# The opening of a two-block transformer kernel rebuilt: c cast by transposes, token-major sums of squares, one x block and one weight per step, matmuls of zeros

## The chip, the core and the metric

One core of a Trainium2 chip runs the whole program in one launch. Time is device microseconds of that core; lower is better. The core has five engines with their own instruction streams, each worked off in order: PE (TensorE: matmuls, with PEld for its weight loads), DVE (VectorE), ACT (ScalarE), POOL (GpSimd) and SP (SyncE, which here issues the DMAs). They wait for each other by semaphores.

## The reference, cut to what matters

Two transformer blocks on 512 tokens of width 1024, batch 1, float32. The opening is the head of the first block: the modulation from c, the first norm, and the first projection.

```python
c_act = jax.nn.silu(c)
mod = (c_act @ ada_w[l] + ada_b[l])[:, None, :]          # 1024 -> 6 * 1024
sh_t, sc_t, g_t, sh_c, sc_c, g_c = jnp.split(mod, 6, axis=-1)
h = rms_norm(x, tm_pre_g[l]) * (1.0 + sc_t) + sh_t       # x / sqrt(mean(x^2) + eps) * g
y = token_mixer(h, w_in[l], ...)                         # starts with h @ w_in
```

## The kernel before

Activations lie with features on the partitions: x is 8 blocks `x0[:, j]` of 128 features by 512 tokens. A float32 product is made of three matmuls of the fp32r type: weight and activation are each split into a high part (rounded, by an ACT copy) and a low part (the rest, by a DVE subtraction), and high times high, high times low and low times high are summed in PSUM (`mm3`, L130 to L133; 512 columns each).

The opening stands in the block `with tc.tile_pool(name="st")`. It has no normed x at first: the gain 1 + scale of the modulation is folded into x, the reciprocal root of the mean square is multiplied onto the results later. Ahead of the loop, c is loaded onto all 128 partitions (`cb`, a DMA of 512 KB from a 4 KB row) and put through Silu on ACT; `ccol` is Silu of c as columns, from the small table `vec`.

The first loop runs over the 8 blocks j of x. I call its parts by step:

- product j: one block of `ada` (block 8 + j, 512 KB, one of four `sraw` buffers) is multiplied by `cb` on DVE and summed along the row into one column of `mod` (L347);
- gain j: a one-column DVE instruction makes `gcols` from it (L393);
- high half j on ACT and low half j on DVE: x block j times its gain, split in two (`xg`, L394 and L395);
- weight split j: a 512 KB block of `w1` is split, its high part on ACT and its low part on DVE (L119, L120). Blocks 0 to 4 go through `sraw`, 5 to 7 through three `raw` buffers (`wload`);
- matmuls of step j: `steps` brings the accumulators of the first four weights (`NF = 4`) up to block j. Step 0 has 3 matmuls, step 1 has 9, step 2 has 15, step 3 has 21, step 4 has 12; steps 5 and 6 have no call of their own: their 24 matmuls are written together with step 7's 12, and the scheduler may put them earlier.

In steps 0 to 3 two blocks of x are loaded per step (`XSTEP`), each squared on ACT (L379) and, but for the first, added into `ssx` on DVE (L381): 7 adds of 512 columns. After step 3 the column sums of `ssx` are taken by matmuls (`colsum`, L240), `rsqrt` makes 1/root from them in 12 small DVE instructions after a copy, `rowcast` puts the 4 columns on all partitions by 4 transposes on PE, and an ACT copy brings that to SBUF as `rx`.

After the loop, DVE takes the four accumulators out of PSUM times `rx` (`gq`, `gk`, L411 and L413), and a second loop over j (L417 on) makes the true normed `h`: the shift from `ada` block j (on DVE, but for j = 1, which `ADA_PE` gives to PE as 8 plain float32 matmuls of one column, L422), the normed block `nt` = x times gain times `rx` (L428), its high half on ACT and low half on DVE (L429, L430), and 12 matmuls for four more weights, whose first is into bank `pb`.

The order within an engine is set by the tile framework's scheduler, by the order in which the code is written and by its priorities; it is fixed when the program is built. SP issues the DMAs in order, each when its buffer is free.

## Time and profile before

| | us |
|---|---|
| median of 3 runs | 1601.64 |
| lowest and highest run | 1598.73, 1603.09 |
| the profiled execution, its own time | 1603.05 |
| its span, first to last instruction | 1601.3 |

The profile is of one execution. The span is what the views below cut up; 1.75 us of that execution's time lie around it. A timeline row gives start and duration of an instruction on its engine, so the start of the next row shows its pitch (instructions overlap a little at their ends). What an engine waited for stands in brackets.

### The profile page before, as it was taken

Reading aid. Unit: us, or ns where it says so; the run is one execution under the profiler, and the core shown is the slowest. Engines: PE = TensorE matmul, PEld = TensorE weight load, DVE = VectorE, ACT = ScalarE, POOL = GpSimd, SP = SyncE. Lnnn points to the kernel's source line nnn. Section 1 sums busy time; section 2 is a strip of 40 time slices with the busy share of each in tenths; the row PEclk is TensorE's granted clock in tenths of the full one; section 3 lists DMA queues with packets and bytes.
Section 4 is the critical chain, followed back from the end, with each engine's and each line's share of the span. In section 5 each row is a group of like instructions: output and inputs, shape, how many; then the busy total and the mean of one; then the engine's idle time right before and its main releaser. Section 6 shows DMA issues by size and latency. Waiting matters only on the chain.

```text
span 1601.3 us, 20852 instructions
## 1 busy us (share of the span) xinstructions
PE 1568.9 (98%) x8015; PEld 1316.4 (82%) x8015; DVE 1083.4 (68%) x2066; ACT 677.5 (42%) x1040; POOL 15.9 (1%) x43
## 2 busy tenths in 40 slices
...
GB/s 305 170 53 67 106 115 187 184 170 153 177 169 17 79 97 100 92 100 91 96 134 187 75 66 89 83 93 27 79 152 59 80 100 98 92 104 81 98 113 53
DMA packets 50963, 175.91 MB, mean 110 GB/s; under 512 B 5920, under 2 KB 6192, under 8 KB 50864
## 3 DMA queue, kind: packets, MB, share of 16 engines
...
HBM read 172.46 MB, written 2.10 MB: 109 GB/s over the span
## 4 chain that ended last, share of the span: by engine, by line
PE 90%; DVE 5%; ACT 3%; DMA 1%; issue 1%; SPq 0%; ACTq 0%; DVEq 0%
PE acc L131 23%; PE acc L132 23%; PE acc L133 23%; PE acc L197 3%; PE acc L1340 3%; PE tp L1340 2%; PE pc L1250 1%; PE pa L197 1%; PE pc L197 1%; PE pb L197 1%; PE pb L1340 1%; PE pa L1340 1%; PE pc L1340 1%; DVE lo L120 1%; PE acc L157 1%
## 5 line engine op out<-in xcount | busy, mean ns | idle before, releaser
L120 DVE TENSOR_TENSOR lo<-raw,hi 128x1024 fp32r<-128x1024 f32 (+1 forms) x245 | 296.4, 1211 | 312.0 <-ACT hi L119 307.9
L131 PE MATMUL acc<-hh,hi 128*128 128x512 f32 x1208 | 474.3, 393 | 0.0
L133 PE MATMUL acc<-hh,lo 128*128 128x512 f32 x1208 | 473.1, 392 | 0.0
L132 PE MATMUL acc<-hl,hi 128*128 128x512 f32 x1208 | 473.1, 392 | 0.0
L119 ACT ACTIVATE hi<-raw 128x1024 fp32r<-128x1024 f32 (+1 forms) x245 | 257.1, 1050 | 471.1 <-PE acc L132 352.6
L131 PEld LDWEIGHTS acc<-hh,hi 128*128 128x128 f32 x1208 | 227.7, 189 | 48.9 <-issue 2.0
L132 PEld LDWEIGHTS acc<-hl,hi 128*128 128x128 f32 x1208 | 227.5, 188 | 48.6 <-issue 1.8
L133 PEld LDWEIGHTS acc<-hh,lo 128*128 128x128 f32 x1208 | 227.6, 188 | 47.5 <-issue 0.7
L131 PE MATMUL acc<-act_h,hi 128*128 128x256 f32 (+1 forms) x242 | 80.4, 332 | 0.0
L132 PE MATMUL acc<-act_l,hi 128*128 128x256 f32 (+1 forms) x242 | 80.2, 331 | 0.0
L133 PE MATMUL acc<-act_h,lo 128*128 128x256 f32 (+1 forms) x242 | 80.2, 331 | 0.0
L119 ACT ACTIVATE act_h<-ffe 128x512 fp32r<-128x512 f32 x44 | 27.7, 630 | 102.5 <-DVE ffe L968 102.5
L265 DVE SCALAR_TENSOR_TENSOR raw<-raw,cb 128x1024 f32<-128x1024 f32 x32 | 39.1, 1223 | 40.0 <-DMA raw<-in_ada_dram 40.0
L964 DVE SCALAR_TENSOR_TENSOR ffe<-acc,vec,ffe 128x510 f32<-128x510 f32 x82 | 61.2, 748 | 2.6
L967 ACT ACTIVATE ffe<-ffe 128x512 f32<-128x512 f32 x44 | 27.8, 631 | 79.5 <-DVE ffe L964 79.5
L962 DVE SCALAR_TENSOR_TENSOR ffe<-acc,vec,ffe 128x511 f32<-128x511 f32 x82 | 60.7, 742 | 0.0
L131 PEld LDWEIGHTS acc<-act_h,hi 128*128 128x128 f32 x242 | 46.0, 190 | 4.4
L133 PEld LDWEIGHTS acc<-act_h,lo 128*128 128x128 f32 x242 | 46.0, 190 | 4.3
L132 PEld LDWEIGHTS acc<-act_l,hi 128*128 128x128 f32 x242 | 46.0, 190 | 4.3
L120 DVE TENSOR_TENSOR act_l<-ffe,act_h 128x512 fp32r<-128x512 f32 x44 | 30.3, 690 | 26.5 <-ACT act_h L119 26.5
L808 DVE SCALAR_TENSOR_TENSOR cv<-u,vec,cv 128x512 f32<-128x512 f32 x60 | 43.8, 746 | 0.1
L197 PE MATMUL acc<-hl,hi 128*128 128x256 f32 x144 | 40.2, 285 | 0.0
...
## 6 DMA issues: line engine op xcount, KB each, us to landing
...
```

The source lines that it names most:

```text
L119: A.activation(hi, src, AF.Copy)
L120: V.tensor_sub(lo, src, hi.bitcast(F32))
L131: T.matmul(out, wh_, ah, start=start, stop=False)
L132: T.matmul(out, wh_, al, start=False, stop=False)
L133: T.matmul(out, wl_, ah, start=False, stop=stop)
L197: T.matmul(a, w_, x_, start=(k == 0 and n == 0 and half == 0), stop=(k == KT - 1 and n == 2 and half == 1), skip_group_check=True)
L265: V.scalar_tensor_tensor(raw, raw, 1.0, cb, op0=ALU.mult, op1=ALU.mult, accum_out=mod[:, i:i + 1])
L808: V.scalar_tensor_tensor(cv[:, j], u0[:, j, k:k + 512], htap[:, 2 * k + j:2 * k + j + 1], cv[:, j], op0=ALU.mult, op1=ALU.add)
L962: V.scalar_tensor_tensor(t[:, 1:512], acc[:, 0:511], vcol(taps, 44 + i), t[:, 1:512], op0=ALU.mult, op1=ALU.add)
L964: V.scalar_tensor_tensor(t[:, 2:512], acc[:, 0:510], vcol(taps, i), t[:, 2:512], op0=ALU.mult, op1=ALU.add)
L967: A.activation(e[0], e[0], AF.Silu)
L1340: T.matmul(o, act[a][:, k, t], w[:, n0:n1], start=(k == 0 and i == 0), stop=(k == KF - 1 and i == 2), skip_group_check=True)
```

## The change

- c: the 512 KB DMA of c is gone. Silu of c as columns (`ccol`) is put on all partitions by 8 transposes on PE, each of one column broadcast over 128, into banks `pb` and `pc`; one half is copied to `cb` by ACT, the other by DVE.
- Matmuls of zeros: `warm` issues 3 and 7 plain float32 matmuls of 256 columns of a zeroed tile, before and after the transposes as the code is written. As built, 5 stand ahead of the transposes and 5 behind them.
- Products 3 and 6 (`ada` blocks 11 and 14, added to `ADA_PE`) are made on PE as 8 one-column matmuls each (L414), and the gain reads PSUM.
- Sums of squares: a second copy of x with tokens on the partitions (`xr`, 4 DMAs of 512 KB) is squared on ACT with a sum along the row, in steps 2 to 5. The 8 squares on ACT, the 7 adds on DVE and the column sums on PE are gone. `rsqrt` and `rowcast` stand behind the loop.
- Each step loads one block of x and one of the weights, and the weight split is written ahead of the high and low half.

```diff
--- before.py
+++ after.py
@@ -48,9 +48,8 @@
        "sb0", "sc0", "sx0", "sb1", "sc1", "sx1"]
 NST = 8
 NF = 4
-XSTEP = (2, 2, 2, 2, 0, 0, 0, 0)
-WSTEP = (1, 1, 1, 1, 1, 1, 1, 1)
-ADA_PE = (1,)
+WARM = (3, 7)
+ADA_PE = (1, 11, 14)
 
 PUMP_P, PUMP_V0, PUMP_V1, PUMP_QK, PUMP_G = 4, 8, 10, 3, (0, 0, 0, 0, 0, 12, 12, 12)
 MT2 = ["ik", "iq0", "iq1", "iq2", "iq3", "p0", "p1", "p2", "p3", "v0", "v1", "v2", "v3",
@@ -350,19 +349,37 @@
 
         x0 = xp.tile([128, KT, 512], F32, tag="x", name="x0")
         xg = h
-        nc.sync.dma_start(out=cb, in_=io["c"].broadcast_to([128, D]))
+
+        zero = st.tile([128, 256], F32, name="zero")
+        G.memset(zero, 0.0)
+        idle = bank("tp")
+
+        def warm(n):
+            for _ in range(n):
+                T.matmul(idle[:, 0:256], zero[:, 0:128], zero, start=True, stop=True)
+
+        warm(WARM[0])
         nc.sync.dma_start(out=vec[:, 0:VSTART], in_=io["vec"][:, 0:VSTART])
-        A.activation(cb, cb, AF.Silu)
+        nc.sync.dma_start(out=ident, in_=io["cst"])
         ccol = sm.tile([128, KT], F32, tag="ccol", name="ccol", bufs=1)
         A.activation(ccol, vcols("c", 8), AF.Silu)
         scb1 = sm.tile([128, KT], F32, tag="scb1", name="scb1", bufs=1)
         V.tensor_scalar(scb1, vcols("ada_b", 8, 8), 1.0, None, op0=ALU.add)
+
+        for n in range(2):
+            cp = bank(("pb", "pc")[n])
+            for k in range(4):
+                T.transpose(cp[:, k * 128:(k + 1) * 128], ccol[:, 4 * n + k:4 * n + k + 1].to_broadcast([128, 128]), ident)
+            if n:
+                V.tensor_copy(cb[:, 512:1024], cp)
+            else:
+                A.activation(cb[:, 0:512], cp, AF.Copy)
+        warm(WARM[1])
         wstf = [st.tile([128, NF, 1024], F32R, name=f"wst{n}") for n in range(2)]
         wst = [(wstf[0][:, m], wstf[1][:, m]) for m in range(NF)]
         wst += [(m4(f"whi{m}", F32R)[:, 0:1024], m4(f"wlo{m}", F32R)[:, 0:1024]) for m in range(NF, NST - 3)]
         accs = [bank(t) for t in ("acc", "acc", "acc", "pa", "pb", "pc", "tp")]
         done = [0] * NST
-        ready = 0
 
         def steps(ms, act, j):
             for m in ms:
@@ -371,42 +388,45 @@
                     mm3(accs[m], wst[m][0][:, sl], wst[m][1][:, sl], act[0][:, k], act[1][:, k], k == 0, k == KT - 1)
                 done[m] = j + 1
 
-        ssx = st.tile([128, 512], F32, name="ssx")
-
-        def xload(j):
+
+        ssx = sm.tile([128, 4], F32, tag="ssx", name="ssx", bufs=1)
+
+        def xsquares(b):
+            xr = st.tile([128, 1024], F32, tag="xr", name="xr", bufs=2)
+            nc.sync.dma_start(out=xr, in_=io["xr"][b * 128:(b + 1) * 128])
+            A.activation(xr, xr, AF.Square, accum_out=ssx[:, b:b + 1])
+
+        def wsplit(m):
+            if m < NST - 3:
+                split(wst[m][0], wst[m][1], sraw(io["w1"][m]))
+            else:
+                floor[0] = tc.cur_priority
+                wst.append(wload(io["w1"][m]))
+
+        for j in range(KT):
+            c = 8 + j
+            g = gcols[:, 0, j:j + 1]
+            raw = sraw(io["ada"][c])
             nc.sync.dma_start(out=x0[:, j], in_=io["xT"][:, j])
-            sq = ssx if j == 0 else st.tile([128, 512], F32, tag="sq", name="sq", bufs=2)
-            A.activation(sq, x0[:, j], AF.Square)
-            if j:
-                V.tensor_tensor(ssx, ssx, sq, op=ALU.add)
-
-        nx = 0
-        rx = None
-        for j in range(KT):
-            ada_st(8 + j)
-            for _ in range(XSTEP[j]):
-                xload(nx)
-                nx += 1
-            if j == 0:
-                nc.sync.dma_start(out=ident, in_=io["cst"])
-            g = gcols[:, 0, j:j + 1]
-            V.scalar_tensor_tensor(g, mod[:, 8 + j:9 + j], scb1[:, j:j + 1], vcol("tm_pre_g", j), op0=ALU.add, op1=ALU.mult)
+            if c in ADA_PE:
+                gp = bank("tp")
+                for k in range(KT):
+                    T.matmul(gp[:, 0:1], raw[:, k * 128:(k + 1) * 128], ccol[:, k:k + 1], start=(k == 0), stop=(k == KT - 1))
+                sc = gp[:, 0:1]
+            else:
+                sc = mod[:, c:c + 1]
+                V.scalar_tensor_tensor(raw, raw, 1.0, cb, op0=ALU.mult, op1=ALU.mult, accum_out=sc)
+            V.scalar_tensor_tensor(g, sc, scb1[:, j:j + 1], vcol("tm_pre_g", j), op0=ALU.add, op1=ALU.mult)
+            wsplit(j)
             A.activation(xg[0][:, j], x0[:, j], AF.Copy, scale=g)
             V.scalar_tensor_tensor(xg[1][:, j], x0[:, j], g, xg[0][:, j].bitcast(F32), op0=ALU.mult, op1=ALU.subtract)
-            for _ in range(WSTEP[j]):
-                if ready < NST - 3:
-                    split(wst[ready][0], wst[ready][1], sraw(io["w1"][ready]))
-                else:
-                    wst.append(wload(io["w1"][ready]))
-                ready += 1
+            if j >= 2 and j < 6:
+                xsquares(j - 2)
             if j not in (KT - 3, KT - 2):
-                steps(range(min(ready, NF)), xg, j)
-            if nx == KT and rx is None:
-                pc = bank("tp")
-                colsum(pc, [ssx])
-                V.tensor_copy(s0, pc[:, 0:4])
-                rx = wraw(None)[:, 0:512]
-                A.activation(rx, rowcast(rsqrt(s0, 1.0 / D, 4)), AF.Copy)
+                steps(range(min(j + 1, NF)), xg, j)
+        V.tensor_copy(s0, ssx)
+        rx = wraw(None)[:, 0:512]
+        A.activation(rx, rowcast(rsqrt(s0, 1.0 / D, 4)), AF.Copy)
         for j in range(2):
             V.scalar_tensor_tensor(gq[:, j], accs[j], 0.125, rx, op0=ALU.mult, op1=ALU.mult)
         for j in range(2):
@@ -1393,7 +1413,7 @@
     i = {k: np.asarray(v) for k, v in i.items()}
     a = {}
     a["xT"] = np.ascontiguousarray(i["x"][0].T.reshape(KT, 128, S).transpose(1, 0, 2))
-    a["c"] = np.ascontiguousarray(i["c"])
+    a["xr"] = np.ascontiguousarray(i["x"][0])
     a["ada"] = np.array(i["ada_w"][0].T, order="C").reshape(48, 128, D)
     for j in ADA_PE:
         a["ada"][j] = _tiles(i["ada_w"][0][:, j * 128:(j + 1) * 128])[0]
```

Lines of the code move with it: in the new kernel the product is L418 (L346 in the second loop), the gain L419, the high and low half L421 and L422, the weight split L118 and L119, the matmuls L130 to L132, the normed block L448.

How the built order moves at three places. On PE, the end of step 2's matmuls and what stands behind them, before (`wst` are the split weights, `hh` and `hl` the halves of x, `ssx` the sums of squares):

```order
L131 MATMUL acc<-hh,wst_109 128x512
L132 MATMUL acc<-hl,wst_109 128x512
L133 MATMUL acc<-hh,wst_110 128x512
L131 MATMUL acc<-hh,wst_109 128x512
L132 MATMUL acc<-hl,wst_109 128x512
L133 MATMUL acc<-hh,wst_110 128x512
L240 MATMUL tp<-cst,ssx 128x1 x4
L131 MATMUL acc<-hh,wst_109 128x512 x3
```

The column sums stand there, which the reciprocal root takes. The same place on PE now (`ccol` is Silu of c as columns, `sraw` here the `ada` block 11):

```order
L131 MATMUL acc<-hl,wst_133 128x512 x2
L132 MATMUL acc<-hh,wst_134 128x512
L131 MATMUL acc<-hl,wst_133 128x512
L132 MATMUL acc<-hh,wst_134 128x512 x2
L130 MATMUL acc<-hh,wst_133 128x512
L131 MATMUL acc<-hl,wst_133 128x512
L132 MATMUL acc<-hh,wst_134 128x512
L414 MATMUL tp<-ccol,sraw 128x1 x8
L130 MATMUL acc<-hh,wst_133 128x512 x3
```

Product 3 has come in behind the last nine matmuls of step 2. On DVE, from low half 2 to weight split 3, before:

```order
L395 SCALAR_TENSOR_TENSOR hl<-x_101,gcols,hh 128x512
L120 TENSOR_TENSOR wst_110<-sraw,wst_109 128x1024
L347 SCALAR_TENSOR_TENSOR sraw,mod<-sraw,cb 128x1024
L381 TENSOR_TENSOR ssx<-ssx,sq 128x512
L393 SCALAR_TENSOR_TENSOR gcols<-mod,scb_107,vec 128x1
L381 TENSOR_TENSOR ssx<-ssx,sq 128x512
L395 SCALAR_TENSOR_TENSOR hl<-x_101,gcols,hh 128x512
```

There the gain reads what DVE itself has just made. The same place on DVE now (`tp` is the PSUM bank of product 3):

```order
L119 TENSOR_TENSOR wst_134<-sraw,wst_133 128x1024
L422 SCALAR_TENSOR_TENSOR hl<-x_101,gcols,hh 128x512
L419 SCALAR_TENSOR_TENSOR gcols<-tp,scb_112,vec 128x1
L422 SCALAR_TENSOR_TENSOR hl<-x_101,gcols,hh 128x512
L119 TENSOR_TENSOR wst_134<-sraw,wst_133 128x1024
L418 SCALAR_TENSOR_TENSOR sraw,mod<-sraw,cb 128x1024
```

Product and adds are gone, gain 3 reads PSUM, and low half, weight split and product 4 stand behind it. On DVE, the end of the first loop and the start of the second, before (`raw` is `rx`, `nt` a normed block):

```order
L395 SCALAR_TENSOR_TENSOR hl<-x_101,gcols,hh 128x512
L426 TENSOR_TENSOR mod<-mod,vec 128x1
L428 SCALAR_TENSOR_TENSOR nt<-x_101,gcols,raw 128x512 x2
L120 TENSOR_TENSOR lo<-raw,hi 128x1024 x2
L411 SCALAR_TENSOR_TENSOR e_97<-acc,raw 128x512 x2
```

There the first loop's last low half and the second loop's first shift (`mod`) come ahead of the normed blocks. The same place on DVE now:

```order
L422 SCALAR_TENSOR_TENSOR hl<-x_101,gcols,hh 128x512
L232 SCALAR_TENSOR_TENSOR rs_y<-rs_u,rs_y 128x4
L119 TENSOR_TENSOR lo<-raw,hi 128x1024
L418 SCALAR_TENSOR_TENSOR sraw,mod<-sraw,cb 128x1024
L448 SCALAR_TENSOR_TENSOR nt<-x_101,gcols,raw 128x512
L419 SCALAR_TENSOR_TENSOR gcols<-mod,scb_112,vec 128x1
L448 SCALAR_TENSOR_TENSOR nt<-x_101,gcols,raw 128x512
```

The first row is low half 6; the normed blocks, which need `rx`, now stand ahead of gain 7, and low half 7, the results of the first loop and the first shift follow behind them.

## Rows read from the trace of the kernel before

**Rows 1.** The head of the page and its first part: the span, and of each engine the busy time, its share of the span and its instructions.

```profile
span 1601.3 us, 20852 instructions
...
PE 1568.9 (98%) x8015; PEld 1316.4 (82%) x8015; DVE 1083.4 (68%) x2066; ACT 677.5 (42%) x1040; POOL 15.9 (1%) x43
```

**Rows 2.** Timeline of VectorE (DVE) in step 2 of the first loop, from one product to the next: start, duration, engine, line, operation, tiles, and in brackets the idle time before it with what ended it.

```profile
17.42 1.22 DVE L347 SCALAR_TENSOR_TENSOR sraw<-sraw,cb 128x1024 f32<-128x1024 f32 x1
18.56 0.08 DVE L347 DVE_READ_ACCUMULATOR sraw<-sraw,cb 128x1 f32 x1
18.56 0.69 DVE L381 TENSOR_TENSOR ssx<-ssx,sq 128x512 f32<-128x512 f32 x1
19.17 0.21 DVE L393 SCALAR_TENSOR_TENSOR gcols<-mod,scb,vec 128x1 f32<-128x1 f32 x1
19.36 0.69 DVE L381 TENSOR_TENSOR ssx<-ssx,sq 128x512 f32<-128x512 f32 x1
20.17 0.75 DVE L395 SCALAR_TENSOR_TENSOR hl<-x,gcols,hh 128x512 fp32r<-128x512 f32 x1
21.12 1.23 DVE L120 TENSOR_TENSOR wst<-sraw,wst 128x1024 fp32r<-128x1024 f32 x1 [0.20 <-ACT wst L119]
22.26 1.22 DVE L347 SCALAR_TENSOR_TENSOR sraw<-sraw,cb 128x1024 f32<-128x1024 f32 x1
```

**Rows 3.** The first data, in the timeline of the whole core up to 9 us: SP issues the DMA of c on all partitions, GpSimd (POOL) its large memsets (128x2048 and 128x1024 in one row), and DVE runs the first product and its gain.

```profile
0.80 0.39 SPq L353 DMA_DIRECT2D cb<-in_c_dram  x1
0.83 2.69 POOL L535 MEMSET x1a<- 128x2048 f32 x2
...
7.64 1.23 DVE L347 SCALAR_TENSOR_TENSOR sraw<-sraw,cb 128x1024 f32<-128x1024 f32 x1 [2.22 <-DMA sraw<-in_ada_dram]
...
8.91 0.22 DVE L393 SCALAR_TENSOR_TENSOR gcols<-mod,scb,vec 128x1 f32<-128x1 f32 x1
```

**Rows 4.** Windows: in each stretch (us) the busy time and instructions of PE, PEld, DVE, ACT and POOL, the granted clock of TensorE (1.00 is 2.4 GHz), the DMA engines' share and GB/s.

```profile
8.00:10.00 2.00, 0.00 (x0) 0.00 (x0) 1.54 (x4) 1.74 (x3) 0.00 (x0) 1.00 1.04 419
16.00:18.00 2.00, 2.00 (x5) 1.49 (x5) 1.80 (x3) 1.51 (x3) 0.00 (x0) 1.00 1.02 405
...
46.00:48.00 2.00, 1.82 (x8) 1.47 (x8) 2.00 (x5) 1.11 (x2) 0.00 (x0) 0.83 0.47 121
48.00:50.00 2.00, 2.00 (x6) 1.55 (x5) 2.00 (x4) 0.00 (x0) 0.00 (x0) 0.50 0.99 381
...
160.00:180.00 20.00, 20.00 (x138) 18.29 (x137) 15.48 (x31) 10.45 (x35) 4.12 (x12) 1.00 0.14 47
```

**Rows 5.** Timeline of TensorE (PE) in three places: step 2 of the first loop; the end of the first loop and the start of the second; the end of the second. L247 is the row cast of the reciprocal root, the first row with `pb` is the second loop's first matmul, L422 the products of one-column matmuls (16 instructions for 8 matmuls), L439 what follows the second loop.

```profile
17.58 0.63 PE L132 MATMUL acc<-hl,wst 128*128 128x512 f32 x1
18.01 0.63 PE L133 MATMUL acc<-hh,wst 128*128 128x512 f32 x1
...
34.38 0.65 PE L247 MATMUL tp<-cst,rs_y 128*128 128x128 f32 x4 [0.61 <-DVE rs_y L233]
...
43.75 0.39 PE L131 MATMUL pb<-hh,whi 128*128 128x512 f32 x1
43.98 0.39 PE L131 MATMUL pc<-hh,hi 128*128 128x512 f32 x1
...
44.43 1.84 PE L422 MATMUL tp<-ccol,sraw 128*128 128x1 f32 x16
46.45 0.50 PE L132 MATMUL pb<-hl,whi 128*128 128x512 f32 x1 [0.18 <-DVE hl L430]
...
48.49 0.63 PE L131 MATMUL acc<-hh,hi 128*128 128x512 f32 x1
48.91 0.63 PE L132 MATMUL acc<-hl,hi 128*128 128x512 f32 x1
...
69.30 0.40 PE L439 MATMUL tp<-wst,sh 128*2 128x512 f32 x1
```

**Rows 6.** Timeline of ACT: high half of a block of x, high part of a weight, two squares of x, the copy of the row cast out of PSUM.

```profile
19.41 0.72 ACT L394 ACTIVATE hh<-x,gcols 128x512 fp32r<-128x512 f32 x1 [1.85 <-DVE gcols L393]
20.04 1.04 ACT L119 ACTIVATE wst<-sraw 128x1024 fp32r<-128x1024 f32 x1
20.99 1.14 ACT L379 ACTIVATE sq<-x 128x512 f32<-128x512 f32 x2
...
35.53 0.57 ACT L409 ACTIVATE raw<-tp 128x512 f32<-128x512 f32 x1
```

**Rows 7.** Groups of instructions on ACT by line and shape: the read of an accumulator that follows an activation with a sum (busy us, mean ns).

```profile
L1241 ACT ACTIVATION_READ_ACCUMULATOR e<-e,mn 128x1 f32 x32 | 6.1, 190 | 0.0
```

**Rows 8.** Timeline of DVE: a gain and two dependent small instructions of the reciprocal root, the first normed blocks of the second loop, and the results of the first loop taken out of PSUM.

```profile
28.85 0.22 DVE L393 SCALAR_TENSOR_TENSOR gcols<-mod,scb,vec 128x1 f32<-128x1 f32 x1
28.98 0.15 DVE L231 TENSOR_TENSOR rs_u<-rs_y 128x4 f32<-128x4 f32 x1
29.17 0.17 DVE L232 SCALAR_TENSOR_TENSOR rs_u<-rs_u,rs_s 128x4 f32<-128x4 f32 x1
...
39.31 1.41 DVE L428 SCALAR_TENSOR_TENSOR nt<-x,gcols,raw 128x512 f32<-128x512 f32 x2
...
43.26 1.28 DVE L411 SCALAR_TENSOR_TENSOR e<-acc,raw 128x512 f32<-128x512 f32 x2
```

**Rows 9.** Timeline of PE: two plain float32 matmuls of 512 columns in four instructions.

```profile
79.08 1.98 PE L540 MATMUL tp<-rows,wa 16*128 16x512 f32 x4
```


## The prediction

> **What bounds the kernel now.** I read the page's head first: TensorE (PE) is busy for 98% of the span [rows 1], so over the whole kernel the time is PE's, and an opening that is late by some microseconds is late for good if PE has no slack later. From 160 us on PE is busy for 20.00 of 20 us [rows 4], so there is none. The opening itself is different. In the timeline of DVE, step 2 of the first loop runs from one product at 17.42 to the next at 22.26, a period of 4.84 us with 0.20 us of idle time in it [rows 2]: DVE sets the pace there, and PE waits. DMA is also full (405 and 419 GB/s, shares of 1.02 and 1.04 [rows 4]), but its data are there when DVE asks. The mark to watch is the first matmul of the second loop, at 43.75 us; what follows the second loop starts at 69.30, 25.55 us later [rows 5]. If that mark moves by d, the kernel moves by about d.
>
> **The change part by part, as a walk along DVE.** DVE works in order, and the build fixes the order shown in the section on the change. So I walk along it with the pitches of the rows: product to gain 1.27 us, gain to next 0.13, weight split 1.14, low half 0.67 [rows 2, 3, 8].
>
> *Front.* The first product starts at 7.64 now, when its `ada` block lands, which stands behind c's 512 KB in the queue [rows 3]. Without c it lands 1.3 us earlier at 405 GB/s, at 6.3. But `cb` now comes out of five matmuls of zeros, eight transposes and two copies from PSUM. No row shows a matmul of zeros; the nearest is a plain float32 matmul of 512 columns, 0.99 us each [rows 9], so 0.5 us for 256 columns, or 1.0 at half the clock. GpSimd fills 3072 columns in 2.69 us [rows 3], so 256 are ready by about 1.1 us. Five of them end between 3.6 and 6.1, eight transposes (four took 0.65 us [rows 5]) take 1.3 to 2.6, a copy 0.6 [rows 6]. With the waits between, the first product starts between 5.9 and 9.5. I take 6.7, a quarter of the way up, since half the clock is the shorter part of the rows of PE; that is 0.9 us earlier than before.
>
> *Steps 0 to 2.* Without the adds a step is 1.27 + 0.13 + 1.14 + 0.67 = 3.2 us, and 3.25 with small waits, in place of 4.84. Three of them end at 6.7 + 9.75 = 16.45; before, low half 2 ended at 20.17 + 0.75 = 20.9 [rows 2]. So the change is 4.5 us ahead here.
>
> *Gain 3.* It reads product 3 from PE, where that product stands behind the last nine matmuls of step 2, which low half 2 releases. At the full clock, 2.4 GHz, a matmul has a pitch of 0.23 us, at 1.2 GHz 0.43 [rows 5]: 2.05 us for nine, or 3.85; I take the full clock, since the zeros and two steps have run before. Then the 16 instructions of the product take 1.84 us [rows 5]. Gain 3 can run at 16.45 + 2.05 + 1.84 + 0.1 = 20.5 (22.3 at half the clock). DVE stands for 4.0 us, and low half 3, weight split 3 and product 4 stand behind it. The product that was saved costs 1.27 us.
>
> *Steps 3 to 5.* DVE now has no other work while ACT makes the high half (0.72 us [rows 6]), and ACT makes high half, weight split and a square in a row. From gain 3 to the end of weight split 3: 3.1 us, until 23.6. Steps 4 and 5: 1.40 for product and gain, 0.85 wait for the high half, 0.67, 0.27 wait for the split's high part, 1.14, together 4.4 us each, until 32.4. The squares on ACT (1.1 us by the two halves of the row, and 0.19 for the read of the sum [rows 6, 7]) fit: 0.65 + 0.95 + 1.25 = 2.9 us of ACT in 4.4. The last square ends just then.
>
> *Gain 6 and the root.* Copy and three instructions of the root, each 0.2 us after the last [rows 8], end at 33.2. Gain 6 waits for product 6, which stands behind the 12 matmuls of step 5: gain 5 at 29.3, low half 5 until 30.9, eight matmuls more until 32.9, 1.84 for the product: 34.9. DVE stands for 1.7 us. The rest of the root, nine instructions in a chain, with low half 6 between them, ends at 37.3; weight split 6 at 38.4, product 7 at 39.7.
>
> *rx.* The row cast stands on PE behind step 6's matmuls. Low half 6 ends at 37.2; eight matmuls after it take 1.8 us, or 3.4 at half the clock. The nearest row is what follows product 1 in the second loop: 16 one-column instructions, then a granted clock of 0.50, 1.2 GHz, in 48 to 50 us [rows 4]. The same kind of product stands here, so I take 3.4. With the transposes (0.65) and ACT's copy (0.57 [rows 5, 6]) `rx` is there at 42.0. The normed block stands next on DVE, ahead of gain 7, so DVE stands for 2.3 us.
>
> *To the mark.* Two normed blocks and gain 7 (1.4 us), constants, weight split 7, low half 7 until 45.6; product 0 of the second loop until 47.0; four results out of PSUM at 0.64 us [rows 8], the last of them when PE has finished (eight matmuls behind low half 7, until 47.5 or 49.1), until 49.8; the shift, high half on ACT 0.8: the second loop's first matmul at 50.9. That is 50.9 - 43.75 = 7.1 us later. In the second loop the same instructions follow in the same place, with product 1 and its slow stretch, so I carry 25.5 us.
>
> *What costs nothing.* The saved DMA of c (512 KB) and the added ones (2 MB) are hidden: 12.2 MB must have landed by x block 7, which at 405 GB/s [rows 4] is 30 us and ends near 33, and the walk wants it at 38.4. If that cover went, at below 0.33 MB per us, DMA would set the time. The memset on POOL and the second five zeros lie in PE's idle time before the first high half.
>
> **Sum.** 1603.05 + 7.1 = 1610.2 for the profiled execution, span 1601.3 and 1.75 around it; the median is 1.4 below that execution, so 1601.64 + 7.1 = **1608.7 us**.
>
> **Rivals.**
>
> *All at the full clock.* If PE stays at 2.4 GHz throughout, `rx` comes 1.6 us earlier, and with a first product at 5.9 another 0.8 is saved: +4.7, 1606.3 us. The clock of 0.50 behind product 1 [rows 4] speaks against it for the stretch behind product 6; a step 3 to 5 less tight than on paper speaks against the front. This would read as no change, as would any smaller sum down to a gain of 4.8 us: 0.3% of the time (4.8 us) is about what a measurement of this kernel can tell from no change.
>
> *Half the clock in steps 0 to 6.* In step 2 the matmuls now have the pitch of half the clock, 0.43 us [rows 5], although the clock column shows 1.00 there [rows 4]; I go by the pitch. If the zeros do not change that, gain 3 comes 1.8 us later, the front up to 1 us later, steps 5 and 7 another 0.5: 7.1 + 3.3 = 10.4, 1612 us. The Trainium skill, TensorE: Matmul & The Clock Gate, section Loop structure matters more than you think, says that bursts of matmuls with waits between them run at the low clock. The pitch in step 2 agrees with it; by that rule the zeros buy nothing that outlasts the next wait.
>
> *The saving reaches PE.* On the other side: if products 3 and 6 are ready when DVE asks, then the seven adds (0.61 pitch) and two products (1.27) leave DVE, 6.8 us with the front's 0.9 on top, 7.7 in all. DMA then sets the floor: x block 7 at 33, its halves and matmuls and the four results until 38.5, which is 5.2 us before 43.75: 1596.4 us. It decides if product 3 is done by 16.45; but nine matmuls that need low half 2 stand ahead of it, so only a different order or data that come late for DVE anyway would hide it. The Trainium skill, DMA: Bandwidth & Descriptors, section Specifications, gives about 358 GB/s as what memory feeds one core; the windows show 405 and 419 [rows 4], so the measurement decides. By the page's figure the floor would be near 37 us and this rival would gain only some 1 us.
>
> **How the numbers follow.** The forecast, gain 3 and gain 6 and `rx` late by PE: 0.55, 1606.5 to 1611. Half the clock in the opening: 0.20, up to 1613. All at the full clock or an equal mix: 0.15, around 1605. The saving reaches PE: 0.10, 1596. The range of 8 in 10 is 1603 to 1613: it leaves out the gain, some of the middle case, and the late end. Slower by over 0.3%: 0.55 + 0.20 = 0.75; within: 0.15; faster: 0.10.
>
> **What would show it.** In the new profile: DVE idle before gain 3 (L419 from `tp`) for some 4 us and before gain 6 for 1 to 2, ended by PE L414; idle before the first `nt` (L448), ended by ACT's copy of the row cast; 3.3 us between the first products; the first matmul into `pb` near 51. It would be wrong if the product on PE comes ahead of what DVE asks, so that those idle times are missing and `pb` starts near 39; if DVE waits for DMA instead, the cover of the added loads is gone; if `pb` is at 51 and the time is unchanged, the kernel has slack between 51 and 160 us that I did not see.

## The result, and the profile after

The changed kernel takes 1611.53 us (median of 4 runs, 1610.95 to 1614.25), the kernel before, on the same chip, 1602.37 us (4 runs): a ratio of 1.0064, 95% interval 1.0052 to 1.0076. It is slower by 9.2 us, where 7.1 were forecast. The profiled execution took 1611.54 us, with a span of 1609.8.

The first places to look are the two marks of TensorE: the first matmul into `pb`, and what follows the second loop (L459). The timeline of TensorE of the changed kernel:

```profile
19.58 1.84 PE L414 MATMUL tp<-ccol,sraw 128*128 128x1 f32 x16
22.49 1.65 PE L130 MATMUL acc<-hh,wst 128*128 128x512 f32 x3 [1.06 <-ACT hh L421]
...
35.63 1.84 PE L414 MATMUL tp<-ccol,sraw 128*128 128x1 f32 x16
...
45.99 1.65 PE L130 MATMUL acc<-hh,wst 128*128 128x512 f32 x3 [2.42 <-ACT hh L421]
...
51.18 0.63 PE L132 MATMUL pa<-hh,wst 128*128 128x512 f32 x1
53.41 0.51 PE L130 MATMUL pb<-hh,whi 128*128 128x512 f32 x1 [1.60 <-ACT hh L449]
...
78.74 0.40 PE L459 MATMUL tp<-wst,sh 128*2 128x512 f32 x1
```

Against [rows 5] the mark moved from 43.75 to 53.41, 9.66 us; the second loop takes 25.33 us where it took 25.55; L459 moved by 9.44. Behind L459 nothing changed: 1609.8 - 78.74 = 1531.1 us to the end, 1601.3 - 69.30 = 1532.0 before. So the whole loss lies ahead of 53.41. The two windows from the first product to the mark show on which side of VectorE (DVE) it lies; columns as in [rows 4], the third pair of a busy time with its count is DVE. Of the kernel before:

```profile
7.64:43.75 36.11, 28.62 (x109) 20.23 (x109) 33.63 (x71) 18.35 (x25) 0.00 (x0) 1.00 0.89 321
```

and of the changed kernel, with three windows whose granted clock matters:

```profile
7.01:53.41 46.40, 37.56 (x140) 28.05 (x138) 32.16 (x65) 19.05 (x26) 0.00 (x0) 0.78 0.82 317
...
24.00:26.00 2.00, 2.00 (x6) 1.58 (x5) 1.96 (x4) 0.42 (x2) 0.00 (x0) 0.50 1.02 415
...
40.00:42.00 2.00, 2.00 (x6) 1.60 (x6) 2.00 (x2) 0.00 (x0) 0.00 (x0) 0.50 0.09 35
...
48.00:50.00 2.00, 2.00 (x6) 1.60 (x6) 1.94 (x5) 0.00 (x0) 0.00 (x0) 0.50 0.00 0
```

DVE's busy time fell from 33.63 to 32.16 us, its idle time rose from 36.11 - 33.63 = 2.48 to 46.40 - 32.16 = 14.24. With the first product 0.63 earlier: -0.63 - 1.47 + 11.76 = 9.66, the shift of the mark. DVE's timeline says where it stands:

```profile
9.19 1.22 DVE L119 TENSOR_TENSOR wst<-sraw,wst 128x1024 fp32r<-128x1024 f32 x1 [0.69 <-ACT wst L118]
...
16.72 0.75 DVE L422 SCALAR_TENSOR_TENSOR hl<-x,gcols,hh 128x512 fp32r<-128x512 f32 x1
21.46 0.22 DVE L419 SCALAR_TENSOR_TENSOR gcols<-tp,scb,vec 128x1 f32<-128x1 f32 x1 [3.99 <-PE tp L414]
22.47 0.75 DVE L422 SCALAR_TENSOR_TENSOR hl<-x,gcols,hh 128x512 fp32r<-128x512 f32 x1 [0.79 <-ACT hh L421]
23.41 1.23 DVE L119 TENSOR_TENSOR wst<-sraw,wst 128x1024 fp32r<-128x1024 f32 x1 [0.20 <-ACT wst L118]
...
37.51 0.22 DVE L419 SCALAR_TENSOR_TENSOR gcols<-tp,scb,vec 128x1 f32<-128x1 f32 x1 [3.45 <-PE tp L414]
...
44.30 0.75 DVE L448 SCALAR_TENSOR_TENSOR nt<-x,gcols,raw 128x512 f32<-128x512 f32 x1 [2.11 <-ACT raw L429]
...
51.84 0.69 DVE L433 TENSOR_TENSOR e<-pa,raw 128x512 f32<-128x512 f32 x1 [0.16 <-PE pa L132]
52.45 0.15 DVE L446 TENSOR_TENSOR mod<-mod,vec 128x1 f32<-128x1 f32 x1
```

The three stands of the forecast are there: 3.99 us before gain 3, 3.45 before gain 6, 2.11 before the first normed block. In steps 3 to 5 DVE waits 0.79 us each time for ACT to make the high half, and 0.20 us for the high part of the weight. The last row is the other thing to see: the add that completes shift 0 stands behind all four results, and high half 0 and the mark wait for it, with TensorE idle for 1.60 us.

### The profile page after: what moved, and what is told of

It is laid out like the page before. It is cut to its first block, busy times and chain, and to the rows that moved or that the text cites. A ratio compares the mean times of both kernels' runs of the same rounds, so it can differ in the third digit from the quotient of the medians.

```text
span 1609.8 us, 20953 instructions
## 1 busy us (share of the span) xinstructions
PE 1583.1 (98%) x8067; PEld 1329.0 (83%) x8067; DVE 1079.2 (67%) x2056; ACT 677.0 (42%) x1040; POOL 16.1 (1%) x44
## 4 chain that ended last, share of the span: by engine, by line
PE 92%; DVE 4%; ACT 3%; issue 1%; DMA 1%; SPq 0%; ACTq 0%; DVEq 0%
PE acc L130 23%; PE acc L131 23%; PE acc L132 23%; PE acc L196 3%; PE acc L1360 3%; PE tp L1360 2%; PE pc L1270 1%; PE pc L196 1%; PE pa L196 1%; PE pb L196 1%; PE pa L1360 1%; PE pb L1360 1%; PE pc L1360 1%; PE acc L156 1%; DVE lo L119 1%
## 5 line engine op out<-in xcount | busy, mean ns | idle before, releaser
L119 DVE TENSOR_TENSOR lo<-raw,hi 128x1024 fp32r<-128x1024 f32 (+1 forms) x245 | 296.6, 1211 | 320.1 <-ACT hi L118 314.9
L130 PE MATMUL acc<-hh,hi 128*128 128x512 f32 x1208 | 473.5, 392 | 0.0
L132 PE MATMUL acc<-hh,lo 128*128 128x512 f32 x1208 | 472.5, 391 | 0.0
L118 ACT ACTIVATE hi<-raw 128x1024 fp32r<-128x1024 f32 (+1 forms) x245 | 257.1, 1050 | 469.9 <-PE acc L131 354.7
L130 PEld LDWEIGHTS acc<-hh,hi 128*128 128x128 f32 x1208 | 227.1, 188 | 48.7 <-issue 2.0
L132 PEld LDWEIGHTS acc<-hh,lo 128*128 128x128 f32 x1208 | 227.3, 188 | 47.7 <-issue 0.7
L130 PE MATMUL acc<-act_h,hi 128*128 128x256 f32 (+1 forms) x242 | 80.5, 332 | 0.0
L132 PE MATMUL acc<-act_h,lo 128*128 128x256 f32 (+1 forms) x242 | 80.2, 331 | 0.0
L118 ACT ACTIVATE act_h<-ffe 128x512 fp32r<-128x512 f32 x44 | 27.7, 630 | 102.5 <-DVE ffe L988 102.5
L130 PEld LDWEIGHTS acc<-act_h,hi 128*128 128x128 f32 x242 | 46.0, 190 | 4.4
L132 PEld LDWEIGHTS acc<-act_h,lo 128*128 128x128 f32 x242 | 46.0, 190 | 4.2
L119 DVE TENSOR_TENSOR act_l<-ffe,act_h 128x512 fp32r<-128x512 f32 x44 | 30.4, 690 | 26.6 <-ACT act_h L118 26.6
L196 PE MATMUL acc<-hh,lo 128*128 128x256 f32 x144 | 40.5, 287 | 0.0
```

The source lines that it names most:

```text
L118: A.activation(hi, src, AF.Copy)
L119: V.tensor_sub(lo, src, hi.bitcast(F32))
L130: T.matmul(out, wh_, ah, start=start, stop=False)
L132: T.matmul(out, wl_, ah, start=False, stop=stop)
L196: T.matmul(a, w_, x_, start=(k == 0 and n == 0 and half == 0), stop=(k == KT - 1 and n == 2 and half == 1), skip_group_check=True)
```

## Experiments

Read from the trace so far: DVE stands for TensorE (**theory A**), TensorE runs at half clock behind the one-column products (**B**), and what DVE has to do between the end of step 7 and the mark is late or stands in a bad order (**C**). All twelve runs in one table: median, ratio to the kernel before on the same chip with its 95% interval, and from one profiled execution the mark, the length of the second loop and the start of what follows it. The runs were made on several chips, on which the kernel before took 1600.98 to 1602.37 us; the ratios are free of that. The profiled execution is not always the median one: that of e4 took 1618.08 us, of e5 1608.73, of e7 1617.29, of e8 1603.34, of e12 1605.22. So the mark and the median of one row need not belong together.

| kernel | median us | ratio (interval) | mark | second loop | follows at |
|---|---|---|---|---|---|
| before | 1602.37 | 1 | 43.75 | 25.55 | 69.30 |
| changed | 1611.53 | 1.0064 (1.0052 to 1.0076) | 53.41 | 25.33 | 78.74 |
| e1_unread | 1609.27 | 1.0041 (1.0029 to 1.0053) | 47.97 | 28.35 | 76.32 |
| e2_no_products | 1608.19 | 1.0036 (1.0024 to 1.0048) | 46.10 | 28.52 | 74.62 |
| e3_rx_ready | 1612.18 | 1.0057 (1.0038 to 1.0076) | 47.87 | 29.68 | 77.55 |
| e4_no_zeros | 1612.60 | 1.0069 (1.0052 to 1.0085) | 55.80 | 28.60 | 84.40 |
| e5_products_dve | 1612.94 | 1.0072 (1.0056 to 1.0088) | 48.22 | 29.23 | 77.45 |
| e6_none_pe | 1607.75 | 1.0036 (1.0023 to 1.0049) | 52.21 | 24.80 | 77.01 |
| e7_zeros_step7 | 1613.50 | 1.0080 (1.0068 to 1.0093) | 55.19 | 28.47 | 83.66 |
| e8_root_early | 1605.86 | 1.0029 (1.0020 to 1.0038) | 46.16 | 24.62 | 70.78 |
| e9_shift0_first | 1607.77 | 1.0040 (1.0027 to 1.0053) | 49.88 | 24.29 | 74.17 |
| e10_root_shift_first | 1602.14 | 1.0002 (0.9993 to 1.0011) | 41.57 | 28.42 | 69.99 |
| e11_before_products | 1605.13 | 1.0019 (1.0009 to 1.0029) | 45.62 | 23.74 | 69.36 |
| e12_low0_first | 1601.60 | 0.9997 (0.9988 to 1.0005) | 43.59 | 26.57 | 70.16 |

**e1_unread.** The products stay on TensorE, the gains don't read them:

```diff
                 for k in range(KT):
                     T.matmul(gp[:, 0:1], raw[:, k * 128:(k + 1) * 128], ccol[:, k:k + 1], start=(k == 0), stop=(k == KT - 1))
-                sc = gp[:, 0:1]
+                sc = mod[:, 9:10]
```

> TensorE still makes the two one-column products of steps 3 and 6 in their places, but nobody reads them: gains 3 and 6 take a sum that is ready since step 1 (so two gains are wrong numbers, and the work of a product is left out on VectorE as well). Theory A, VectorE stands for products that queue behind matmuls: its idle times of 3.99 and 3.45 us ahead of these gains go, some of it comes back as waits on later things, the mark (first matmul into pb, 53.41 us now) comes 4 to 7 us earlier and the time falls by 4 to 7 us against the changed kernel. Rival B, TensorE's clock: the 16 one-column instructions are still followed by some 6 us at 1.2 GHz, and it is these matmuls that are late; then the time falls by less than 2 us.

The mark came 5.4 us earlier, as theory A says, but the time fell by 2.3 us only: the second loop took 28.35 us in place of 25.33. In TensorE's timeline of this run one sees why:

```profile
47.97 0.80 PE L130 MATMUL pb<-hh,whi 128*128 128x512 f32 x1 [2.37 <-ACT hh L449]
...
49.84 3.41 PE L442 MATMUL tp<-ccol,sraw 128*128 128x1 f32 x16
```

TensorE had idle time ahead of the mark, the granted clock was 0.50 from 50 to 54 us, and product 1 of the second loop took 3.41 us where it took 2.14 in the changed kernel. So the earlier mark is in part given back in the second loop. But this run does not hold theories A and B apart, because the low clock behind product 3 went together with the stand:

```profile
21.29 1.84 PE L414 MATMUL tp<-ccol,sraw 128*128 128x1 f32 x16
23.00 0.94 PE L130 MATMUL acc<-hh,wst 128*128 128x512 f32 x3
```

High half 3 is there when the product ends, TensorE goes on at once, and the granted clock is 1.00 from 18 to 46 us. In the changed kernel TensorE stood for 1.06 us behind the same product and then ran at 0.50.

**e2_no_products.** The one-column matmuls of steps 3 and 6 go as well:

```diff
             if c in ADA_PE:
-                gp = bank("tp")
...
+                sc = mod[:, 9:10]
```

> As the run with unread products, and the one-column matmuls of steps 3 and 6 are left out on TensorE too (gains 3 and 6 read the ready sum of step 1). Against the unread products this takes 2 x 1.84 us of TensorE and whatever the clock does after them. Theory A: TensorE has idle time in the opening, so at most 1.5 us more than the run before gains. Rival B: the granted clock stays at 1.00 where it was 0.50 from 22 to 28 us, 12 matmuls at 0.43 us become 12 at 0.23, and after product 6 the same, so 3 to 5 us more than with unread products.

1.1 us less than e1 in the median, with overlapping intervals; the mark 1.9 us earlier, the second loop 28.52 us. By the bound set ahead (at most 1.5 us for A, 3 to 5 for B) this would speak against B, but B's premise was gone: the clock behind the products was at 1.00 in e1 already. What the low clock of the changed kernel costs apart from the stands is thus not shown. Stand, product and clock together are worth some 3 us: with both products gone altogether, some 6 of the 9 us remain.

**e3_rx_ready.** Squares, root and row cast are left out, `rx` is a constant:

```diff
-            if j >= 2 and j < 6:
-                xsquares(j - 2)
...
-        A.activation(rx, rowcast(rsqrt(s0, 1.0 / D, 4)), AF.Copy)
+        rx = st.tile([128, 512], F32, name="rx")
+        G.memset(rx, 1.0)
```

> Sums of squares, root and row cast are left out: rx is a constant that is filled before the first loop, so four loads of x by tokens, four squares on ScalarE, 14 small VectorE instructions and the row cast go, and the first two normed blocks can run at any time. Rival C, the root that now comes after step 5 is what makes the opening late: the mark comes 5 us or more earlier, and the time falls by as much. Theory A: the stands before gains 3 and 6 stay, so the time falls by 1 to 3 us only: the 2.11 us wait of the first normed block goes, but TensorE still ends step 7 late.

The time did not move beyond its interval, which neither theory had said. The mark came 5.5 us earlier and the second loop took 29.68 us: ahead of the mark DVE did the four results and two products for shifts in a row, from 42.08 us to the add of shift 0 at 46.83, while TensorE was idle for 4.92 us. The late root is not by itself the cause.

**e4_no_zeros.**

```diff
-WARM = (3, 7)
+WARM = (0, 0)
```

> No matmuls of zeros: both groups are left out, nothing else. All theories: the transposes of c run when vec and the identity have landed, so the first product starts within 0.4 us of 7.01. If the zeros bought clock for steps 0 to 2, these run with a pitch of 0.43 us for longer than the 10 to 15 us seen with zeros, low half 2 and gain 3 come up to 1.8 us later, and the time rises by 1 to 2 us; if they bought nothing, steps 1 and 2 show the same clock as with zeros and the time stays within 0.7 us.

The first product started at 6.34 in place of 7.01 us, 0.7 earlier where at most 0.4 was given, and the median is 1.1 us higher with intervals that overlap: the zeros are worth nothing that can be measured. In the trace they did show: without them the matmuls keep the pitch of half the clock until 18.1 us, with them until 14.7, though here step 0 also lost 2.91 us to a weight that landed late. The trace teaches one thing more. From the mark on this run has the order and the 1.60 us of idle time of the changed kernel, and yet its second loop took 28.60 us, at a granted clock of 0.50 from 50 to 66 us. So the length of that loop can differ by 3 us with the same order and the same idle time ahead of it.

**e5_products_dve.** Products 3 and 6 back on DVE, the rest of the change kept:

```diff
-ADA_PE = (1, 11, 14)
+ADA_PE = (1,)
```

> Products 3 and 6 go back to VectorE (1.27 us each), the rest of the change stays. Theory A as it was: no stand for PE, the mark 3 to 5 us earlier than 53.41 and the time lower by as much. Theory A with the clock behind it (what the runs with unread and without products suggest: their mark came 5.4 and 7.3 us earlier, but the second loop took 28.4 and 28.5 us in place of 25.3): TensorE has idle time ahead of the mark, the one-column product of the second loop runs at half clock (3.41 us in place of 1.84 to 2.14) and the matmuls behind it too, so 2 to 3 us are given back and the time falls by only 0 to 3 us; it stays over 1604.

The most telling miss: the stands are gone, the mark is at 48.22, and the median is 1612.94, no better than the changed kernel. Theory A in its first form falls. The six times lie in two groups, 1608.73 to 1610.43 and 1615.45 to 1615.87 us, and the trace is of the fastest. Its second loop took 29.23 us. DVE ahead of the mark, and TensorE's row of the mark, in this run:

```profile
42.12 1.28 DVE L431 SCALAR_TENSOR_TENSOR e<-acc,raw 128x512 f32<-128x512 f32 x2
43.31 0.68 DVE L433 TENSOR_TENSOR e<-acc,raw 128x512 f32<-128x512 f32 x1
43.91 0.68 DVE L433 TENSOR_TENSOR e<-pa,raw 128x512 f32<-128x512 f32 x1
...
44.97 1.21 DVE L346 SCALAR_TENSOR_TENSOR sraw<-sraw,cb 128x1024 f32<-128x1024 f32 x1
...
46.12 1.22 DVE L346 SCALAR_TENSOR_TENSOR sraw<-sraw,cb 128x1024 f32<-128x1024 f32 x1
...
47.26 0.15 DVE L446 TENSOR_TENSOR mod<-mod,vec 128x1 f32<-128x1 f32 x1
```

```profile
48.22 0.80 PE L130 MATMUL pb<-hh,whi 128*128 128x512 f32 x1 [5.00 <-ACT hh L449]
```

TensorE has nothing to do for 5.00 us while DVE makes four results, the constants, the product for shift 0 and, ahead of the add that TensorE waits for, the product for a later shift.

**e6_none_pe.** Shift 1 on DVE too:

```diff
-ADA_PE = (1, 11, 14)
+ADA_PE = ()
```

> No one-column product on TensorE at all: 3 and 6 on VectorE as in the run before it, and shift 1 of the second loop too. If the second loop is long because of the one-column product and the half clock behind it, the second loop falls from some 28 us to 24 to 25.5 us, and the time is 2.5 to 4 us under that run. If VectorE sets the second loop (a step there is 1.22 + 0.08 + 0.15 + 0.74 + 0.75 us less overlaps, some 2.7 us, against 12 matmuls at 0.23), the extra 1.27 us shows as an idle time of TensorE and the gain is below 1 us.

The second loop is back at 24.80 us and the median 5.2 us under that of e5, more than the 2.5 to 4 us given: this points to the one-column product in the second loop. In e5 it took 1.84 us, TensorE stood for 1.00 us behind it, and the granted clock fell again, to 0.50 from 58 to 60 us. But the two traces do not show the 5.2 us, since what follows the loop starts at 77.45 and 77.01: here the mark is at 52.21, behind an idle time of 4.36 us, as the build had again put two shift products ahead of the add.

**e7_zeros_step7.** Five more matmuls of zeros, which run ahead of step 7:

```diff
+        idle = bank("tp")
+        warm(5)
         shp = bank("tp")
```

> The changed kernel with five more matmuls of zeros, which the build puts on TensorE behind the row cast and ahead of the matmuls of step 7, where TensorE has an idle time of 2.42 us and comes out of it at 1.2 GHz (granted clock 0.50 from 46 to 52 us). If the clock of step 7 is a term of its own: 1.00 there, the last matmul of step 7 ends up to 2.5 us earlier, the mark follows by 1.5 to 2.5 us and the time falls by 1 to 2.5 us. If VectorE sets the mark anyway (weight split 7, low half 7, product 0 and the four results in a row), the clock rises but the time stays within 0.7 us.

Step 7 ran at a granted clock of 1.00 in place of 0.50, from the row cast to its last matmul 7.2 us in place of 8.8; but the mark still came 9.55 us behind the row cast (10.44 without), after 2.39 us of idle time, and the median rose by 2.0 us, with intervals that overlap. Of the 1.7 us that step 7 gained, 0.9 reached the mark; behind that DVE's results and the add set it.

**e8_root_early.** Products on DVE, sums of squares again from the x blocks, their adds on GpSimd, root behind step 5:

```diff
-ADA_PE = (1, 11, 14)
+XSTEP = (1, 1, 1, 1, 2, 2, 0, 0)
+ADA_PE = (1,)
...
-            xr = st.tile([128, 1024], F32, tag="xr", name="xr", bufs=2)
...
+            sq = ssx if j == 0 else st.tile([128, 512], F32, tag="sq", name="sq", bufs=2)
+            A.activation(sq, x0[:, j], AF.Square)
+            if j:
+                G.tensor_tensor(ssx, ssx, sq, op=ALU.add)
```

> Products 3 and 6 on VectorE, and the sums of squares are again taken from the x blocks of the first loop, with ScalarE's squares as before and the adds on GpSimd instead of VectorE; x blocks come one per step to step 3 and two in steps 4 and 5, and the root follows step 5. No loads of x by tokens; front and zeros stay. VectorE is free of the adds and of all stands: steps of 3.2 us to step 4, the root ends near 35, rx at some 36, the normed blocks need not wait, and nothing stands between the last results of the first loop and the mark: mark at 42 to 45 us, and with TensorE busy up to it the second loop takes 25.5 us as before: 1600 to 1604 us. Rival: GpSimd's adds slow VectorE down or take over 1.5 us each, the root comes later than 38, and the time is over 1606.

1605.86 us, between the two outcomes. In the trace, which is of the fastest of its 11 executions (1603.34 us), the mark comes without idle time of TensorE, at 46.16, and the second loop takes 24.62 us. DVE lost time in a way that only the rival named, as its timeline and GpSimd's show:

```profile
15.62 2.30 DVE L422 SCALAR_TENSOR_TENSOR sraw<-sraw,cb 128x1024 f32<-128x1024 f32 x1
...
19.90 1.22 DVE L422 SCALAR_TENSOR_TENSOR sraw<-sraw,cb 128x1024 f32<-128x1024 f32 x1
...
21.16 1.12 DVE L423 SCALAR_TENSOR_TENSOR gcols<-mod,scb,vec 128x1 f32<-128x1 f32 x1
```

```profile
15.33 1.51 POOL L399 TENSOR_TENSOR ssx<-ssx,sq 128x512 f32<-128x512 f32 x1 [2.77 <-ACT sq L397]
19.90 2.37 POOL L399 TENSOR_TENSOR ssx<-ssx,sq 128x512 f32<-128x512 f32 x1 [3.06 <-ACT sq L397]
```

**e9_shift0_first.** The changed kernel, with nothing but shift 0 written ahead of the results:

```diff
+        ada_st(0)
+        V.tensor_tensor(mod[:, 0:1], mod[:, 0:1], vcol("ada_b", 0), op=ALU.add)
         for j in range(2):
             V.scalar_tensor_tensor(gq[:, j], accs[j], 0.125, rx, op0=ALU.mult, op1=ALU.mult)
...
-            if j in ADA_PE:
+            if j == 0:
+                pass
+            elif j in ADA_PE:
```

> The changed kernel with one move in the code: the product for shift 0 and its add are written ahead of the four results of the first loop, so that the build puts the product (1.22 us) between low half 7 and the first result and the add behind the first result; the products for 3 and 6 stay on TensorE. Theory C, what costs the time is VectorE work that stands between the last matmul of step 7 and the mark while TensorE is idle: the add no longer follows the four results (49.28 to 52.45 us), high half 0 comes some 2.5 us earlier, the mark with it, and the idle time of 1.60 us before it goes, so the time falls by 2 to 4 us against the changed kernel. Rival: the end of the first loop on TensorE (51.8 us) sets the mark by itself; then the time stays within 1 us.

1607.77 us, 3.8 less, in the range that theory C gave, with both products still on TensorE. The add stands behind the first result now and the mark has no idle time before it; the second loop is 24.29 us, at a granted clock of 1.00:

```profile
48.31 0.69 DVE L433 SCALAR_TENSOR_TENSOR e<-acc,raw 128x512 f32<-128x512 f32 x1 [0.17 <-PE acc L132]
48.92 0.15 DVE L431 TENSOR_TENSOR mod<-mod,vec 128x1 f32<-128x1 f32 x1
```

```profile
49.88 0.50 PE L130 MATMUL pb<-hh,whi 128*128 128x512 f32 x1
```

From the first normed block to the mark it is 6.22 us in place of 9.11; the rest of the mark's 3.5 us lies ahead of that, in a stretch that the edit does not touch. Along with the add the build also moved small work on constants (0.65 us) behind the results.

**e10_root_shift_first.** e5 with the root written behind step 5 and shift 0 ahead of the results:

```diff
-ADA_PE = (1, 11, 14)
+ADA_PE = (1,)
...
+            if j == 5:
+                V.tensor_copy(s0, ssx)
+                rx = wraw(None)[:, 0:512]
+                A.activation(rx, rowcast(rsqrt(s0, 1.0 / D, 4)), AF.Copy)
+        ada_st(0)
+        V.tensor_tensor(mod[:, 0:1], mod[:, 0:1], vcol("ada_b", 0), op=ALU.add)
```

> Products 3 and 6 on VectorE, the root written behind step 5 in place of behind the loop, and shift 0 written ahead of the results; squares by tokens, zeros and transposes of c stay. No work is added or taken away against the run with products 3 and 6 on VectorE (1612.9): only the order differs, by which gain 7 and low half 7 come ahead of the end of the root and of weight split 6, and splits 6 and 7 stand behind the results as in the kernel before. Theory C (order ahead of the mark): mark at 41 to 45 us with no idle time of TensorE before it, second loop 24 to 26 us, time 1600 to 1605, 8 us or more under that run. Rival, the work moved to other engines is itself too much (squares on ScalarE, loads by tokens, 0.79 and 0.20 us waits in each step): 1607 or more.

1602.14 us, the time of the kernel before, and 10.8 us under e5, which does the same work (7.1 between the two profiled executions, as e5's is its fastest). DVE now reaches the mark's add ahead of the results, and TensorE goes over into the second loop without a gap:

```profile
37.26 0.22 DVE L419 SCALAR_TENSOR_TENSOR gcols<-mod,scb,vec 128x1 f32<-128x1 f32 x1
...
37.67 1.22 DVE L346 SCALAR_TENSOR_TENSOR sraw<-sraw,cb 128x1024 f32<-128x1024 f32 x1
...
39.48 0.15 DVE L432 TENSOR_TENSOR mod<-mod,vec 128x1 f32<-128x1 f32 x1
...
40.68 1.28 DVE L434 SCALAR_TENSOR_TENSOR e<-acc,raw 128x512 f32<-128x512 f32 x2
```

```profile
41.57 0.49 PE L130 MATMUL pb<-hh,whi 128*128 128x512 f32 x1
...
46.13 0.79 PE L131 MATMUL pb<-hl,whi 128*128 128x512 f32 x1 [1.10 <-DVE hl L455]
```

The second loop still takes 28.42 us: low half 0 now stands behind the results and two weight splits, TensorE waits 1.10 us for it, and the granted clock is 0.50 from 46 to 52 us. The mark gained 6.65 us against e5, what follows the loop 7.46.

**e11_before_products.** The kernel before, with products 3 and 6 on TensorE and nothing else of the change:

```diff
-ADA_PE = (1,)
+ADA_PE = (1, 11, 14)
...
+            if 8 + j in ADA_PE:
+                raw = sraw(io["ada"][8 + j])
...
+                sc = gp[:, 0:1]
+            else:
+                ada_st(8 + j)
+                sc = mod[:, 8 + j:9 + j]
```

> The kernel before with one part of the change alone: products 3 and 6 on TensorE in the first loop. Theory A (VectorE stands for products that queue behind matmuls of the step before): two stands of 1 to 4 us for 2 x 1.27 us saved, and the clock at 0.50 behind each product, so 2 to 6 us slower than the kernel before. Theory C: in the kernel before VectorE is ahead of TensorE by several us at the end of the loop, so a stand uses up that lead first; within 2 us of the kernel before.

3.6 us slower than the kernel before (1605.13 against 1601.53 on the same chip): inside what A said, outside C's 2 us. Gain 3 waits 2.25 us for its product, gain 6 not at all:

```profile
24.82 0.22 DVE L401 SCALAR_TENSOR_TENSOR gcols<-tp,scb,vec 128x1 f32<-128x1 f32 x1 [2.25 <-PE tp L390]
...
36.45 0.22 DVE L401 SCALAR_TENSOR_TENSOR gcols<-tp,scb,vec 128x1 f32<-128x1 f32 x1
```

So the products do cost something by themselves, about a third of the 9.2 us. It is A's number and not A's mechanism: one of the two stands is missing, and the granted clock is 1.00 behind both products. The profiled execution shows only part of it: what follows the second loop starts there at 69.36, as before, but the first product ran at 6.48 in place of 7.64 us, so the opening became 1.2 us longer.

**e12_low0_first.** e10 with low half 0 of the second loop at a higher priority:

```diff
-            V.scalar_tensor_tensor(h[1][:, j], t, sh, h[0][:, j].bitcast(F32), op0=ALU.add, op1=ALU.subtract)
+            with tc.high_priority(offset=60 if j < 1 else 1):
+                V.scalar_tensor_tensor(h[1][:, j], t, sh, h[0][:, j].bitcast(F32), op0=ALU.add, op1=ALU.subtract)
```

> The run with the root and shift 0 first, and one more move: low half 0 of the second loop gets a priority of 60 ahead, by which the build puts it behind the second result and ahead of the two others and of weight splits 6 and 7 (there it stood behind them at 45.34 us, and TensorE waited 1.10 us for it, with a granted clock of 0.50 from 46 to 50 us). Theory C (order at the mark): TensorE gets the low half some 3 us earlier, the idle time of 1.10 us goes, but weight splits 6 and 7 come 1 us later and part of it goes there; the first matmul of what follows the second loop comes 0.5 to 2 us earlier than 69.99, time 1600.2 to 1601.7, which beats the run before it and may just beat the kernel before. Rival: the splits are what TensorE waits for next; the same time as the run before it or up to 1 us more.

1601.60 us: the time is inside what was given, but neither e10 nor the kernel before can be told from it, and the mechanism missed. Low half 0 came 1.7 us earlier and the wait of 1.10 us went, but the mark came at 43.59, TensorE stood for 0.79 us ahead of block 1 of that loop instead, with a granted clock of 0.50 from 50 to 52 us, and what follows the loop started at 70.16, not earlier than 69.99. No version that was run beats the kernel before.

## Why the prediction was right, point by point

**The bound.** Right: the rest of the kernel kept its length to 1 us, and the mark's shift came through.

**Front.** The first product at 7.01, forecast 6.7. Not in the walk: weight 0 landed late, ACT waited 1.72 us for it, and weight split 0 on DVE stood 0.69 us, so step 0 took 3.99 us. Steps 1 and 2 took 3.19 and 3.20 (3.25). Low half 2 ended 1.0 us late, at 17.47.

**Gain 3.** Stand 3.99 us, forecast 4.0, with the nine matmuls at the full clock, as chosen. Steps 4 and 5 took 4.36 and 4.37 us (4.4).

**Gain 6: the term that was mis-sized.** It came at 37.51, forecast 34.9: 1.0 us is the front's, carried along, and the stand is 3.45 us where 1.7 was forecast. The walk charged half the clock behind product 6 but not behind product 3; there the granted clock was 0.50 from 22 to 28 us, the first 14 or so matmuls of step 3 went at a pitch of 0.43 us, and product 6 could start only at 35.63, forecast 32.9. The late front and the longer stand make up the 2.5 us by which the mark came later than the forecast's 50.9.

**rx and the mark.** The stand before the first normed block is 2.11 us (2.3), at half clock as assumed; from that block to the mark 9.1 us (8.9). The second loop took 25.33 us (25.5).

**What the walk did not say, and the runs show.** A walk along one order prices that order; it doesn't say what the time would be without a wait. The rows made three stands look like the cause, 9.55 us in sum. With both products ready or away (e1, e2) only 2.3 and 3.3 us came back, with the products on DVE (e5) nothing, with `rx` ready (e3) nothing. So far as the prediction took the stands for the cause, its number came out near by luck: where a stand went, something else in the same order took its place.

What the same work costs in another order was 3.8 us less on the changed kernel (e9) and 10.8 us less with the products on DVE (e10 against e5). In e5 nearly the whole loss, then, is the order that the build made of the new code: gain 7 and the normed blocks behind the root's late end, and the product and the add of shift 0 behind the four results, so that TensorE runs dry ahead of the mark. For the changed kernel itself 3.8 of the 9.2 us are shown to be order. The rest is argued: the products on TensorE cost 3.6 us in the old order (e11), and the place of the root may be the remainder, but the run that would tell, e10 with both products on TensorE, was not made. Nor was the root's move apart from that of shift 0.

That the second loop takes 25.5 us was an assumption with a condition: TensorE must come to it busy and not wait at its start. With shift 1 on TensorE and 1.6 to 5.0 us of idle time ahead of the mark, the loop took 28.4 to 29.7 us in the traces of e1 to e5 and e7. The changed kernel got away with 25.33 after 1.60 us, e11 with 23.74 after 0.90; and e10 took 28.42 with no idle time ahead of the mark, but with a wait of 1.10 us just behind product 1. These are single executions; e4, with the order and the idle time of the changed kernel, shows that they can differ by 3 us.

**Why the saved adds bring nothing even in the good order.** In e10 low half 2 ends at 17.74, 3.2 us ahead of the kernel before, and product 3 starts 4.6 us ahead (17.66 against 22.26, [rows 2]). At the mark 2.2 us of that are left, and the second loop, 2.9 us longer, takes these. Where the first part goes, DVE and ACT show, in e10:

```profile
17.66 1.22 DVE L418 SCALAR_TENSOR_TENSOR sraw<-sraw,cb 128x1024 f32<-128x1024 f32 x1
...
20.25 0.75 DVE L422 SCALAR_TENSOR_TENSOR hl<-x,gcols,hh 128x512 fp32r<-128x512 f32 x1 [1.11 <-ACT hh L421]
21.78 1.23 DVE L119 TENSOR_TENSOR wst<-sraw,wst 128x1024 fp32r<-128x1024 f32 x1 [0.78 <-ACT wst L118]
23.23 1.23 DVE L418 SCALAR_TENSOR_TENSOR sraw<-sraw,cb 128x1024 f32<-128x1024 f32 x1 [0.23 <-DMA sraw<-in_ada_dram]
...
25.51 0.75 DVE L422 SCALAR_TENSOR_TENSOR hl<-x,gcols,hh 128x512 fp32r<-128x512 f32 x1 [0.79 <-ACT hh L421]
...
28.11 1.23 DVE L418 SCALAR_TENSOR_TENSOR sraw<-sraw,cb 128x1024 f32<-128x1024 f32 x1 [0.23 <-DMA sraw<-in_ada_dram]
```

```profile
19.49 0.72 ACT L421 ACTIVATE hh<-x,gcols 128x512 fp32r<-128x512 f32 x1 [1.75 <-DMA x<-in_xT_dram]
20.68 1.06 ACT L118 ACTIVATE wst<-sraw 128x1024 fp32r<-128x1024 f32 x1 [0.47 <-DMA sraw<-in_w_dram]
...
24.75 0.72 ACT L421 ACTIVATE hh<-x,gcols 128x512 fp32r<-128x512 f32 x1 [1.60 <-DVE gcols L419]
```

Steps 3 and 4 take 5.57 and 4.88 us, no less than the 4.84 of the kernel before with its two adds. In step 3 it is DMA: ACT waits 1.75 us for block 3 of x and 0.47 for the weight, and DVE waits for ACT. In step 4 ACT has been idle for 1.60 us when the gain comes; DVE then waits 0.79 us for the high half, a place that the second add of a step filled in the kernel before [rows 2], and another 0.39 and 0.23 us for the weight's high part and for DMA. In the changed kernel, where no wait for DMA is seen from step 3 on, the same step takes 4.36 us.

**DMA.** "Costs nothing" held in the changed kernel but for the 0.69 us of weight 0: ACT also waited 1.48 and 1.10 us for weights 1 and 2, but DVE did not. It did not hold where the stands are gone: in e10 ACT and DVE wait for DMA as above, with 400 GB/s and a DMA share of 1.02 in the window 6.95 to 41.57 (321 GB/s and 0.89 in the kernel before). The Trainium skill, DMA: Bandwidth & Descriptors, section Specifications, gives about 358 GB/s; the trace does not agree here either.

**The rivals.** The one in which the saving reaches PE did not come about. The one with half the clock in steps 0 to 6 came about in part, and the measured 9.2 us lie nearer to its 10.4 than to the forecast's 7.1: the granted clock was 0.50 from 12 to 14 us, so the zeros outlasted no wait, as that rival said, and again from 22 to 28, from 40 to 42 and from 46 to 52. But its main term failed, since the nine matmuls ahead of product 3 ran at the full clock.
